# Two engines for one subtraction: every second half unit of split weights moves from VectorE to GpSimd in three stages of a two-model kernel

## The chip, the cores and the metric

The kernel is one program on one core of a Trainium2 chip. It is written in a tile language: the code names tiles and engines, and a scheduler then sets the order in which each engine gets its instructions. The metric is device time in microseconds for one execution, lower is better. Before the change the median of three runs is 2018.29 us (2015.76 to 2020.21).

In the text PE is TensorE (matrix multiplies), DVE is VectorE, ACT is ScalarE, POOL is GpSimd and SP is the engine that issues the DMAs. "L108" is line 108 of the kernel before.

## What is computed

Two small transformer networks run one behind the other, each with two layers, width 1024, 256 tokens, batch 1, all in float32. Only `x` of both is returned. Cut to its skeleton:

```
first block (x and a context ctx, modulated by c):
  layer 0: short convolution mixer on x and ctx, then SwiGLU FFN (hidden 2816) on x and ctx
  layer 1: neighbourhood attention of x (16 heads, bias, plus all of ctx), then SwiGLU FFN on x
second block (on the x above, with a memory of 256 rows):
  layer 0: FFN1 (x + 0.5 swiglu), mixer A (gated linear attention, 4 heads, plus 4 memory heads), FFN2
  layer 1: FFN1,                  mixer B (windowed attention, 16 heads, plus 4 memory heads), FFN2
```

Every one of these stages is a few products `activations @ weights`, and the weights are read from HBM as the stage needs them (345.68 MB are read in all).

## The kernel before

**Split products.** A float32 product is made of three fast passes. Every operand is split in two parts: `hi` is the value rounded to the fast format (`F32R`), `lo` is what is left. A product is then hi·hi + hi·lo + lo·hi. In the mixers and the attention `mm3` (L249, L250, L251) issues these three matmuls; in the FFNs `pair_unit` (L318, L320) does the same with wider tiles.

**The weight stream.** `WeightStream` brings the weights in units of 128 partitions x 1024 columns. `load` (L91) issues the DMA of a unit into one of five buffers `wraw`. `_split` makes the two parts: ACT copies `wraw` to `whi` (L107), and VectorE subtracts `whi` from `wraw` and writes `wlo` (L108). There are four buffers of each. `take` hands out a unit and first splits every unit up to two ahead of the one that is now used. The unit is cut into pieces of `self.width` columns; the FFN function `ffn_pairs` sets `width` to 1024 (one piece) and sets it back to 512 (two pieces, the two half units of the title) at its end. The stages with half units that matter here are the attention (`attention_block`), mixer A (`mixer_a`) and mixer B (`mixer_b`).

**What else VectorE does in these three stages.** It makes the `lo` part of every activation (`Net.split`, L264 and L267), normalises heads (`head_rstd` and `newton`: a reduction at L1022 and then a chain of a dozen instructions on 8 to 16 columns, L277 to L281; `head_scale`, L1042), finds the row maxima of the scores (L1150, L1826), scales the softmax rows (L1157, L1388, L1846) and adds the products to the residual `X` (L562, L1424, L1438). PE transposes what comes out of these (L1092 for queries, L1632 and L1853 for others), so PE waits for VectorE at those points.

**What sets the order.** In each of the three stages two generators are woven together by `weave`: one issues the projections (weights), the other the heads. From the program that comes out, the scheduler then makes one list per engine. Engines work their lists in order and wait for each other by semaphores. GpSimd has almost nothing in its list: it clears a few tiles (`memset`), among them at the start of mixers A and B (L1464 to L1471, L1707 to L1714).

Of the kernel before, what the change touches and what calls it, by code (L numbers as in the profile page):

```python
# [8 lines left out]
F32 = mybir.dt.float32  # L9
# [3 lines left out]
ALU = mybir.AluOpType  # L13
# [54 lines left out]
class WeightStream:  # L68
# [4 lines left out]
    def __init__(self, net, es, specs, raw_bufs, split_bufs, ahead):  # L73
# [10 lines left out]
        self.ready = []  # L84
        self.width = 512

    def load(self, upto):
        while self.loaded < min(upto, len(self.specs)):
            ap, nk, ncol, _ = self.specs[self.loaded]
            raw = self.raw_pool.tile([P, self.UNIT], F32, name="wraw", tag="raw")  # L90
            self.nc.sync.dma_start(raw[:, : nk * ncol].rearrange("p (k c) -> p k c", k=nk), ap)  # L91
            self.raw.append((raw, nk, ncol))
            self.loaded += 1

    def _split(self):
        self.load(self.split + self.raw_bufs)
        raw, nk, ncol = self.raw.pop(0)
        n = nk * ncol
        v = lambda t: t[:, :n].rearrange("p (k c) -> p k c", k=nk)
        if self.specs[self.split][3]:  # L100
            self.ready.append((v(raw), None, nk, ncol))
        else:
            hi = self.split_pool.tile([P, self.UNIT], F32R, name="whi", tag="hi")
            lo = self.split_pool.tile([P, self.UNIT], F32R, name="wlo", tag="lo")
            for c0 in range(0, n, self.width):
                cs = slice(c0, min(n, c0 + self.width))
                self.nc.scalar.copy(hi[:, cs], raw[:, cs])  # L107
                self.nc.vector.tensor_tensor(lo[:, cs], raw[:, cs], hi[:, cs].bitcast(F32), ALU.subtract)  # L108
            self.ready.append((v(hi), v(lo), nk, ncol))
        self.split += 1  # L110

# [51 lines left out]
class Net:  # L163
# [463 lines left out]
    def ffn_pairs(self, hp, x2, rows, evac, first):  # L627

        nc = self.nc
        s2 = hp.tile([P, HB, 2, T], F32R, name="s2")
        wide = lambda tag, bufs: hp.tile([P, 4, T], F32, name=tag, tag=tag, bufs=bufs)
        two = lambda t: t.rearrange("p (c t) -> p c t", c=2)
        self.half_banks(first)
        self.ws.width = WeightStream.UNIT
        env = {}

        def hidden(g, ps):

            low = wide("low", 1)
            nc.scalar.copy(low, ps[:, :, 1, :])
            h = wide("h", 2)
            nc.vector.tensor_tensor(h, ps[:, :, 0, :], low, ALU.add)
            if rows is not None:
                nc.vector.tensor_tensor(h, h, env["R"][:, None, :].to_broadcast([P, 4, T]), ALU.mult)
            yield
            sg = two(self.tmp())
            nc.scalar.activation(sg, h[:, 0:2, :], AF.Silu)
            s = two(self.tmp())  # L650
            nc.vector.tensor_tensor(s, h[:, 2:4, :], sg, ALU.mult)
            yield
            self.split(s2[:, 2 * g : 2 * g + 2, 0, :], s2[:, 2 * g : 2 * g + 2, 1, :], s)
            yield

        behind = iter(())
        ps = self.group_banks()
        for g in range(HB // 2):
            after = None
            for u in range(4):  # L660
                unit = self.ws.take()
                self.pair_unit(unit, [ps[:, u // 2 * 2 + c] for c in range(2)], x2, u % 2 * 4, KB)
                next(behind, None)
                if g == 0 and u == 1:
                    after = self.group_banks()
                    if rows is not None:
                        env["R"] = rows(after[:, 0].rearrange("p a t -> p (a t)"))
            behind = hidden(g, ps)
            next(behind)
            if g < HB // 2 - 1:  # L670
                ps = after if after is not None else self.group_banks()
        for j in range(4):
            if j % 2 == 0:
                i = self.turn
                self.turn = 1 - i
                self.open_half(i, "po")
            pss = [self.pg[i].tile([P, 2, T], F32, name="po", tag="po") for _ in range(2)]
            done = 0
            while done < HB:
                unit = self.ws.take()  # L680
                self.pair_unit(unit, pss, s2, done, HB)
                next(behind, None)
                done += unit[2]
            for c in range(2):
                evac(2 * j + c, pss[c])
        self.ws.width = 512
# [359 lines left out]
def attention_block(net):  # L1046

    nc, tc, a = net.nc, net.tc, net.a
    xh, xl = net.xa
    k8 = list(range(8))  # L1050
    net.ctx_pool.close()
    net.banks(3, 5)
    with ExitStack() as es:
        op = es.enter_context(tc.tile_pool(name="attn1", bufs=1))
        heads_pool = es.enter_context(ExitStack())
# [390 lines left out]
def mixer_a(net, x2, acc, gain):  # L1446
    nc, tc = net.nc, net.tc
    xh, xl = x2[:, :, 0, :], x2[:, :, 1, :]
    net.banks(4, 4)
    k8 = list(range(8))  # L1450
    with tc.tile_pool(name="mixa", bufs=1) as mp:
        yh = mp.tile([P, 12, T], F32R, name="yh")
# [236 lines left out]
def mixer_b(net, x2, acc, gain):  # L1689
    nc, tc = net.nc, net.tc  # L1690
    xh, xl = x2[:, :, 0, :], x2[:, :, 1, :]
    net.banks(4, 4)
    with tc.tile_pool(name="mixb", bufs=1) as mp:
        yh = mp.tile([P, 12, T], F32R, name="yh")
        yl = mp.tile([P, 12, T], F32R, name="yl")
# [191 lines left out]
def network(tc, a, out, es):  # L1887
# [27 lines left out]
    net.open_x = open_x  # L1915
    net.next_x = next_x
    x2, acc = attention_block(net)
    net.rope = net.cp.tile([P, 32], F32, name="rope")
    x2, acc = ffn2(net, x2, acc, net.p("mix_g0"), 1, rope=True)
    x2, acc = mixer_a(net, x2, acc, net.p("ffn2_g0"))  # L1920
    x2, acc = ffn2(net, x2, acc, net.p("ffn1_g1"), 0)
    x2, acc = ffn2(net, x2, acc, net.p("mix_g1"), 1)
    x2, acc = mixer_b(net, x2, acc, net.p("ffn2_g1"))
    ffn2(net, x2, acc, None, 0, last=True)

# [110 lines left out]
```

## Time and profile before

The times are those of the profiled execution. The span is what the profiler saw; the execution itself took 2018.19 us, 1.89 us more than its span.

| | value |
|---|---|
| median of three runs | 2018.29 us |
| profiled execution, its own time | 2018.19 us |
| its span | 2016.3 us |
| PE busy | 1992.2 us (99%) |
| DVE busy | 1497.7 us (74%) |
| ACT busy | 1025.2 us (51%) |
| POOL busy | 5.1 us (0%) |
| TensorE clock granted | 0.999 |
| moved from HBM | 345.68 MB at a mean of 172 GB/s |

The share of an engine over the whole span hides stages of different kind: the convolution block lies before 602 us, the attention at 602 to 834 us, mixer A at 1198 to 1342 us, mixer B at 1707 to 1835 us, and FFNs between them and after. In rows that tell who waited, "PE pa L1092 <- DVE t L1042: 2.4, 2, 1.2" reads: PE stood idle ahead of the instruction of line 1092 until the DVE instruction of line 1042 had ended; 2.4 us in total, 2 times, the longest 1.2 us.

### The profile page before, as it was taken

Reading aid. Unit: us, or ns where it says so; the run is one execution under the profiler, and the core shown is the slowest. Engines: PE = TensorE matmul, PEld = TensorE weight load, DVE = VectorE, ACT = ScalarE, POOL = GpSimd, SP = SyncE. Lnnn points to the kernel's source line nnn. Section 1 sums busy time; section 2 is a strip of 40 time slices with the busy share of each in tenths; the row PEclk is TensorE's granted clock in tenths of the full one; section 3 lists DMA queues with packets and bytes.
Section 4 is the critical chain, followed back from the end, with each engine's and each line's share of the span. In section 5 each row is a group of like instructions: output and inputs, shape, how many; then the busy total and the mean of one; then the engine's idle time right before and its main releaser. Section 6 shows DMA issues by size and latency. Waiting matters only on the chain. (4 is left out here: it accounts for less than half of the span.)

```text
span 2016.3 us, 32186 instructions
## 1 busy us (share of the span) xinstructions
PE 1992.2 (99%) x12454; PEld 1763.9 (87%) x12454; DVE 1497.7 (74%) x2626; ACT 1025.2 (51%) x1681; POOL 5.1 (0%) x26
## 2 busy tenths in 40 slices
PE   9999999999999999999999999999999999999999
PEld 6788988888899999888888899998888888988888
DVE  5898777767478779766687767787767776888774
ACT  4433532123355656655455547655555555675552
POOL 0000000000000000000000000000000000000000
PEclk9999999999999999999999999999999999999999
DMA  7665455667354334566666565556566656425654
GB/s 252 218 195 182 126 185 170 195 233 249 117 182 127 90 118 125 158 193 188 190 186 193 180 188 136 153 175 195 187 183 198 189 178 188 142 79 177 188 179 136
DMA packets 319273, 348.84 MB, mean 173 GB/s; under 512 B 12624, under 2 KB 307664, under 8 KB 319120
## 3 DMA queue, kind: packets, MB, share of 16 engines
q1 hardware_dynamic: 319120, 346.78, 55.8%
q8 instruction: 98, 1.61, 0.3%
q14 instruction: 55, 0.45, 0.1%
HBM read 345.68 MB, written 1.05 MB: 172 GB/s over the span
## 5 line engine op out<-in xcount | busy, mean ns | idle before, releaser
L108 DVE TENSOR_TENSOR wlo<-wraw,whi 128x512 fp32r<-128x512 f32 (+1 forms) x777 | 702.5, 918 | 341.3 <-ACT whi L107 336.3
L107 ACT CAST whi<-wraw 128x512 fp32r<-128x512 f32 (+1 forms) x777 | 608.9, 804 | 678.6 <-issue 182.9
L318 PE MATMUL pg<-x,whi 128*128 128x512 f32 x1408 | 383.7, 394 | 0.8 <-DVE x L267 0.8
L318 PEld LDWEIGHTS pg<-x,whi 128*128 128x128 f32 x1408 | 239.3, 188 | 33.3 <-DVE x L267 3.2
L318 PE MATMUL po<-s,whi 128*128 128x512 f32 x880 | 241.7, 393 | 0.0
L320 PEld LDWEIGHTS pg<-x,wlo 128*128 128x128 f32 x1408 | 213.5, 188 | 29.4
L320 PE MATMUL pg<-x,wlo 128*128 128x256 f32 x1408 | 219.7, 278 | 0.0
L249 PE MATMUL pm<-xh,whi 128*128 128x512 f32 (+1 forms) x576 | 217.8, 380 | 1.0 <-ACT xh L263 1.0
L250 PE MATMUL pm<-xl,whi 128*128 128x512 f32 (+1 forms) x576 | 217.6, 378 | 0.0
L251 PE MATMUL pm<-xh,wlo 128*128 128x512 f32 (+1 forms) x576 | 217.4, 378 | 0.0
L486 DVE SCALAR_TENSOR_TENSOR ada_acc<-wraw,sil,ada_acc 128x1024 f32<-128x1024 f32 x112 | 140.8, 1280 | 38.9 <-DMA wraw<-in_w_ada 38.3
L318 PEld LDWEIGHTS po<-s,whi 128*128 128x128 f32 x880 | 148.0, 188 | 17.2
L320 PEld LDWEIGHTS po<-s,wlo 128*128 128x128 f32 x880 | 136.4, 188 | 20.3
L320 PE MATMUL po<-s,wlo 128*128 128x256 f32 x880 | 140.9, 278 | 0.0
L249 PEld LDWEIGHTS pm<-xh,whi 128*128 128x128 f32 x576 | 108.1, 188 | 21.9 <-ACT xh L263 1.9
L250 PEld LDWEIGHTS pm<-xl,whi 128*128 128x128 f32 x576 | 108.4, 188 | 20.5 <-DVE xl L264 0.9
L251 PEld LDWEIGHTS pm<-xh,wlo 128*128 128x128 f32 x576 | 108.3, 188 | 19.9
L249 PE MATMUL pm<-sh,whi 128*128 128x256 f32 (+1 forms) x352 | 113.4, 322 | 0.0
L251 PE MATMUL pm<-sh,wlo 128*128 128x256 f32 (+1 forms) x352 | 113.2, 322 | 0.0
L250 PE MATMUL pm<-sl,whi 128*128 128x256 f32 (+1 forms) x352 | 112.7, 320 | 0.0
L251 PE MATMUL pm<-whi,xl 128*128 128x256 f32 x352 | 98.2, 279 | 0.0
L318 PE MATMUL pg<-xh,whi 128*128 128x512 f32 x352 | 96.0, 394 | 1.9 <-DVE xh L264 1.9
(442 smaller groups left out, 3391.1 us busy)
## 6 DMA issues: line engine op xcount, KB each, us to landing
wraw<-in_ffn_w_in SPq DMA_DIRECT2D x264, 512.0 KB, 3.7
wraw<-in_ffn_w_out SPq DMA_DIRECT2D x128, 512.0 KB, 3.5
wraw<-in_w_ada SPq DMA_DIRECT2D x96, 512.0 KB, 4.7
wraw<-in_a_w_in SPq DMA_DIRECT2D x28, 512.0 KB, 3.7
wraw<-in_attn_w_qkv SPq DMA_DIRECT2D x24, 512.0 KB, 4.1
wraw<-in_conv_w_in SPq DMA_DIRECT2D x18, 512.0 KB, 3.9
wraw<-in_ffn_w_out SPq DMA_DIRECT2D x28, 256.0 KB, 2.8
wraw<-in_b_w_in SPq DMA_DIRECT2D x14, 512.0 KB, 3.8
```

The source lines that it names most:

```text
L107: self.nc.scalar.copy(hi[:, cs], raw[:, cs])
L108: self.nc.vector.tensor_tensor(lo[:, cs], raw[:, cs], hi[:, cs].bitcast(F32), ALU.subtract)
L249: mm(ps, ah, bh, start=first, stop=False)
L250: mm(ps, ah, bl, start=False, stop=False)
L251: mm(ps, al, bh, start=False, stop=last)
L318: self.nc.tensor.matmul(pss[c], hi[:, kk, cs], x2[:, done + kk], start=done + kk == 0, stop=False)
L320: self.nc.tensor.matmul(pss[c][:, 0, :], lo[:, kk, cs], x2[:, done + kk, 0, :], start=False, stop=done + kk == nblocks - 1)
L486: nc.vector.scalar_tensor_tensor(accs[v], w, c, accs[v], ALU.mult, ALU.add)
```

## The change

`WeightStream` gets a list `engines`, at first only VectorE. In `_split` the i-th piece of a unit is subtracted by `engines[i % len(engines)]`. The attention and both mixers set the list to VectorE and GpSimd; `ffn_pairs` sets it back to VectorE alone. With pieces of 512 columns a unit has two, so the first half stays on VectorE and the second goes to GpSimd.

```diff
@@ WeightStream.__init__
         self.width = 512
+        self.engines = [net.nc.vector]
@@ WeightStream._split
-            for c0 in range(0, n, self.width):
+            for i, c0 in enumerate(range(0, n, self.width)):
                 cs = slice(c0, min(n, c0 + self.width))
                 self.nc.scalar.copy(hi[:, cs], raw[:, cs])
-                self.nc.vector.tensor_tensor(lo[:, cs], raw[:, cs], hi[:, cs].bitcast(F32), ALU.subtract)
+                self.engines[i % len(self.engines)].tensor_tensor(lo[:, cs], raw[:, cs], hi[:, cs].bitcast(F32), ALU.subtract)
@@ Net.ffn_pairs
         self.ws.width = WeightStream.UNIT
+        self.ws.engines = [nc.vector]
@@ attention_block
     net.banks(3, 5)
+    net.ws.engines = [nc.vector, nc.gpsimd]
@@ mixer_a and mixer_b
     net.banks(4, 4)
+    net.ws.engines = [nc.vector, nc.gpsimd]
```

The lines added shift the numbers: L108 is L110 in the changed kernel, L264 is L266, L277 to L281 are L279 to L283, L1022 is L1025, L1042 is L1045, L1846 is L1852.

What the scheduler makes of it: VectorE's list gets 106 instructions shorter, GpSimd's gets 106 subtractions. PE has the same 12314 rows of matmul in another order at some places of these three stages, ACT the same rows with some order changed, and SP three pairs of DMAs exchanged.

GpSimd's list from its first memset to the start of mixer A, in the changed kernel (`wlo`, `wraw`, `whi` are the lo part, the loaded weights and the hi part; `rb` is cleared in mixer A):

```order
L802 MEMSET z_118 128x516
L802 MEMSET z_119 128x516
L110 ISA
L110 TENSOR_TENSOR wlo<-wraw,whi 128x512 x2
L1065 MEMSET bias 128x256
L110 TENSOR_TENSOR wlo<-wraw,whi 128x512 x39
L1469 MEMSET rb 64x256
```

The 41 subtractions up to here are those of the attention and the first of mixer A; before the change only the memsets were in this list. The instruction `ISA` ahead of the first subtraction is new too. The list at mixer B, in the changed kernel:

```order
L110 TENSOR_TENSOR wlo<-wraw,whi 128x512 x40
L1713 MEMSET vh 128x1024
L1713 MEMSET vl 128x1024
L1720 MEMSET pth_17428 128x2x128
L1720 MEMSET ptl_17430 128x2x128
L1720 MEMSET pth_17429 128x2x128
L1720 MEMSET ptl_17431 128x2x128
L110 TENSOR_TENSOR wlo<-wraw,whi 128x512 x25
```

The 25 subtractions of mixer B stand behind the six memsets; all but one of the 40 ahead of them belong to mixer A.

VectorE's list in the attention, where the queries of one quarter of the heads are normalised (`qr_s`, `qr_g`, `qr_t`, `qr_r` are the statistics of the heads, `ptl` the lo part of the softmax rows of another quarter), before:

```order
L1022 TENSOR_REDUCE qr_s<-t 128x8
L108 TENSOR_TENSOR wlo<-wraw,whi 128x512
L1025 TENSOR_SCALAR qr_s<-qr_s 128x8
L108 TENSOR_TENSOR wlo<-wraw,whi 128x512
L277 TENSOR_SCALAR qr_g<-qr_s 128x8
L264 TENSOR_TENSOR ptl<-pa,pth 128x4x128
L279 SCALAR_TENSOR_TENSOR qr_t<-qr_g 128x8
L280 TENSOR_TENSOR qr_t<-qr_t,qr_s 128x8
L281 SCALAR_TENSOR_TENSOR qr_g<-qr_t,qr_g 128x8
```

and in the changed kernel:

```order
L1025 TENSOR_REDUCE qr_s<-t 128x8
L110 TENSOR_TENSOR wlo<-wraw,whi 128x512
L1028 TENSOR_SCALAR qr_s<-qr_s 128x8
L279 TENSOR_SCALAR qr_g<-qr_s 128x8
L281 SCALAR_TENSOR_TENSOR qr_t<-qr_g 128x8
L266 TENSOR_TENSOR ptl<-pa,pth 128x4x128
L282 TENSOR_TENSOR qr_t<-qr_t,qr_s 128x8
L283 SCALAR_TENSOR_TENSOR qr_g<-qr_t,qr_g 128x8
```

One of the two subtractions that stood inside the chain from L1022 to L281 is gone from VectorE's list, and the `ptl` split stands one step later.

VectorE's list in mixer B, at the first softmax rows (`bst` holds the row statistics, `t` the rows that PE transposes next), before:

```order
L108 TENSOR_TENSOR wlo<-wraw,whi 128x512
L1846 TENSOR_SCALAR t<-t,bst 128x128 x2
L108 TENSOR_TENSOR wlo<-wraw,whi 128x512
L1424 TENSOR_TENSOR X<-pm,X 128x512
L1838 TENSOR_TENSOR bst<-bst 128x4
L108 TENSOR_TENSOR wlo<-wraw,whi 128x512
L1839 RECIPROCAL bst<-bst 128x4
L264 TENSOR_TENSOR ptl_17430<-pa,pth_17428 128x384
L1846 TENSOR_SCALAR t<-t,bst 128x128 x2
```

and in the changed kernel:

```order
L1428 TENSOR_TENSOR X<-pm,X 128x512
L1852 TENSOR_SCALAR t<-t,bst 128x128 x2
L110 TENSOR_TENSOR wlo<-wraw,whi 128x512
L1844 TENSOR_TENSOR bst<-bst 128x4
L1845 RECIPROCAL bst<-bst 128x4
L1852 TENSOR_SCALAR t<-t,bst 128x128 x2
```

Between the first and the second pair of L1846 there stood two subtractions, one addition to `X` and one `ptl` split; now one subtraction stands there.

More of the change, by code (lines that the diff above doesn't have):

```diff
@@ L1692, in mixer_b @@
     net.banks(4, 4)
+    net.ws.engines = [nc.vector, nc.gpsimd]
     with tc.tile_pool(name="mixb", bufs=1) as mp:
```

## The prediction

> **What bounds the kernel now.** I read the page first, then the waits of PE by stage, then the windows of the three stages that the change touches.
>
> ```profile
> span 2016.3 us, 32186 instructions
> PE 1992.2 (99%) x12454; PEld 1763.9 (87%) x12454; DVE 1497.7 (74%) x2626; ACT 1025.2 (51%) x1681; POOL 5.1 (0%) x26
> ```
>
> PE works for 1992.2 of 2016.3 us, and the change takes no matmul away. So all that any change on VectorE can win is in the 24.1 us in which PE stands. How much of that lies in the three stages is told by the windows (columns: window, its length, then the busy time of PE, PEld, DVE, ACT and POOL with their instructions, the granted clock, the DMA share, GB/s), here the attention, mixer A and mixer B:
>
> ```profile
> 602.00:834.00 232.00, 224.57 (x1858) 213.17 (x1856) 188.01 (x508) 142.14 (x295) 0.31 (x1) 1.00 0.38 115
> 1198.00:1342.00 144.00, 141.82 (x1182) 137.93 (x1181) 115.72 (x322) 91.57 (x205) 0.71 (x13) 1.00 0.54 158
> 1707.00:1835.00 128.00, 122.82 (x1012) 115.92 (x1010) 110.73 (x375) 88.93 (x230) 2.85 (x6) 0.99 0.39 119
> ```
>
> PE stands 7.43, 2.18 and 5.18 us there, 14.8 us together: 0.73% of the span is the ceiling. VectorE is busy for 81, 80 and 87% of these stages. What PE waited for, in the same three windows and in the same order (line, then whose end released it: us in total, times, the longest):
>
> ```profile
> PE pa L1092 <- DVE t L1042: 2.4, 2, 1.2
> PE pg L318 <- DVE xh L264: 1.9, 2, 1.7
> PE pa L381 <- DVE acc L574: 0.8, 1, 0.8
> PE pa L1167 <- DVE rc_g L281: 0.6, 1, 0.6
> PE pm L250 <- DVE wlo L108: 0.5, 1, 0.5
> PE pa L1277 <- DVE t L1042: 0.3, 1, 0.3
> PE pa L1118 <- DVE t L1042: 0.2, 1, 0.2
> ...
> PE pa L1632 <- DVE t L1626: 1.8, 4, 0.8
> PE pa L1396 <- DVE t L1388: 0.2, 1, 0.2
> ...
> PE pm L249 <- ACT yh L263: 1.5, 3, 0.7
> PE pa L1853 <- DVE t L1846: 1.3, 1, 1.3
> PE pa L1853 <- ACT t L1844: 1.0, 2, 0.8
> PE pa L1785 <- DVE t L1742: 0.6, 1, 0.6
> PE pa L1396 <- DVE t L1388: 0.2, 1, 0.2
> PE pg L318 <- DVE x L267: 0.2, 1, 0.2
> ```
>
> VectorE is named for 6.7 + 2.0 + 2.3 = 11.0 us. The subtraction itself (`wlo`) is named once, for 0.5 us. The rest is other work of VectorE that came late, and the subtractions matter only because they stand in front of it.
>
> **What the change removes.** These are the subtractions of half units, on VectorE, in the three windows:
>
> ```profile
> L108 DVE TENSOR_TENSOR wlo<-wraw,whi 128x512 fp32r<-128x512 f32 x79 | 52.6, 685 | 7.1 <-ACT whi L107 6.8
> ...
> L108 DVE TENSOR_TENSOR wlo<-wraw,whi 128x512 fp32r<-128x512 f32 x79 | 52.9, 686 | 9.4 <-ACT whi L107 9.0
> ...
> L108 DVE TENSOR_TENSOR wlo<-wraw,whi 128x512 fp32r<-128x512 f32 x51 | 34.0, 685 | 1.4 <-ACT whi L107 1.2
> ```
>
> 106 of them leave VectorE's list, 0.686 us each: 72.7 us of VectorE's 414 us in these stages. How one of them lies on the path is seen at a stall of PE in the attention, first VectorE's own instructions in order of time (start, duration), then the PE row that ended the stall:
>
> ```profile
> 688.61 0.69 DVE L1022 TENSOR_REDUCE qr_s<-t 128x8 f32<-128x512 f32 x1 [0.41 <-ACT t L1021]
> 689.21 0.68 DVE L108 TENSOR_TENSOR wlo<-wraw,whi 128x512 fp32r<-128x512 f32 x1
> 689.81 0.17 DVE L1025 TENSOR_SCALAR qr_s<-qr_s 128x8 f32<-128x8 f32 x1
> 689.89 0.69 DVE L108 TENSOR_TENSOR wlo<-wraw,whi 128x512 fp32r<-128x512 f32 x1
> 690.49 0.17 DVE L277 TENSOR_SCALAR qr_g<-qr_s 128x8 int32<-128x8 int32 x1
> ...
> 693.79 0.63 PE L1092 MATMUL pa<-kc,t 128*128 128x128 f32 x4 [1.21 <-DVE t L1042]
> ```
>
> VectorE runs without a gap from 688.61 to the `t` that PE waits for. Two subtractions stand in it; the list of the changed kernel keeps one. So this stall would go from 1.21 to about 0.5 us if nothing else happened. I count the same for each stall that VectorE causes: 0.69 us, or the whole stall where it is shorter. Attention: 1.4 + 0.9 + 0.7 + 0.6 + 0.5 + 0.3 + 0.2 = 4.6. Mixer A: 1.7 + 0.2 = 1.9. Mixer B: 0.7 + 0.6 + 0.2 + 0.2 = 1.7. Together **8.2 us, the gain if GpSimd's work were free**. The 2.5 us for which PE waits for ACT in mixer B stay.
>
> **What the change adds.** 106 subtractions on GpSimd. The trace has no two-input instruction of GpSimd; its nearest row is a memset of the same size:
>
> ```profile
> L799 POOL MEMSET z<- 128x516 f32 x2 | 1.0, 528 | 0.3 <-POOLq L2032 0.3
> ```
>
> A memset passes the tile once, in 0.53 us. A subtraction passes it three times (two reads, one write). So 0.53 us is the lower bound and 3 x 0.53 = 1.58 us the upper; I take two passes, 1.06 us, between them and above VectorE's own 0.686, because reading and writing may overlap but two reads on one engine less so. 106 x 1.06 = 112 us on an engine that is otherwise idle (0.31, 0.71 and 2.85 us in the windows), so by itself this costs nothing. The Trainium skill, "GPSIMD Engine Reference", section 3.1, gives about 2.6 cycles per element at 1.2 GHz for a two-input operation; an estimate from that page is 512 x 2.6 / 1.2 GHz = 1.11 us, and the forecast below would move by 0.3 us.
>
> Is the second half of a unit late at PE? Units are split two ahead; 79 pieces, that is about 40 units, in 232 us make 5.9 us per unit, so a half unit has some 11 us until PE needs it, and in mixer B (51 pieces in 128 us) some 10 us. Against this stand 1.06 or 1.58 instead of 0.69 us: nothing. The one wait that the change puts in front of subtractions is at the head of mixer B, where 25 of them are queued behind six memsets that wait for the FFN's last matmul and take 2.85 us; that too is inside 10 us. A `wraw` buffer is free at most 0.9 us later for its next DMA on SP's queue; DMAs are busy for 38 to 54% there, and five buffers cover it. `ISA` and the first use of GpSimd come in the 600 us in which it idles. If such cover were gone, each late unit would cost PE its lateness, 0.4 to 0.9 us. The scheduler also puts some matmuls, DMAs and ACT copies in another order; the trace has no price for that, and I bound it by the longest stall, 1.7 us, on either side, and take 0.
>
> **The open cost: do the two engines hinder each other?** In the trace GpSimd never reads while VectorE works. Let f be the part of GpSimd's time for which VectorE stands still because of it; f is between 0 and 1. Then a moved subtraction gives VectorE 0.69 - f x 1.06 us. I take the middle, f = 0.5, since no row leans to either end: 0.16 us, 23% of full relief. The Trainium skill, "SBUF — State Buffer", section "Who interferes with whom", speaks against the change: a VectorE instruction with two SBUF inputs and a GpSimd instruction that reads SBUF exclude each other for the whole instruction. No row here shows that yet. Half-unit subtractions, `newton` steps and `acc` additions are of that kind, while the splits from PSUM banks (`pa`, `pm`) are not, so by that page f is well above 0 and below 1.
>
> Where f is large, the loss comes in the stretches in which VectorE has no room, or in which PE already stands (the windows as above, then for `wlo` alone: length, PE, PEld, DVE, clock, DMA share, GB/s):
>
> ```profile
> 770.00:810.00 40.00, 38.66 (x314) 35.78 (x314) 38.94 (x120) 25.98 (x55) 0.00 (x0) 1.00 0.44 135
> 1736.00:1768.00 32.00, 31.64 (x269) 30.71 (x268) 31.34 (x96) 21.67 (x50) 0.00 (x0) 1.00 0.44 134
> 1768.00:1800.00 32.00, 28.11 (x222) 24.05 (x221) 26.68 (x124) 25.53 (x86) 0.00 (x0) 0.95 0.21 66
> ...
> 770.00:810.00 40.00, 18.59 (x66) 12.39 (x66) 14.56 (x22) 1.00 0.44 135
> 1736.00:1768.00 32.00, 17.73 (x64) 11.95 (x64) 11.53 (x17) 1.00 0.44 134
> 1768.00:1800.00 32.00, 5.81 (x21) 3.76 (x20) 3.94 (x6) 0.95 0.21 66
> ```
>
> VectorE is busy 38.94 of 40 and 31.34 of 32 us in the first two, and 45 subtractions lie in the three; about 22 move.
>
> **The sum.** The profiled execution took 2018.19 us with a span of 2016.3; 1.89 us lie around the span and stay, and it stands 0.1 us below the median of the runs (2018.29), so I use it for both. 23% of 8.2 us is 1.9 us: 2018.2 - 1.9 = **2016.3 us**.
>
> **The rivals.** *Full relief* (f below 0.33): at f = 0 the whole 8.2 us come, 2010.0 us; at f = 0.33 half of it, 2014.2. For it speaks that no row quoted here shows one engine stretching another's instruction; against it that the moved half runs on GpSimd just when the `newton` steps behind the kept half run on VectorE. Its middle is 2012.
>
> *VectorE stands behind GpSimd* (slower): the break-even is f = 0.69/1.06 = 0.65. Above it each of the 22 moved subtractions in the full stretches lengthens VectorE, one for one on PE: at f = 1 by 0.37 us, 8.2 us in all, 2026.4 us; from f = 0.82 on it is 4 us. If a subtraction took 1.58 us as well, it would be 22 x 0.89 = 19.6 us, 2037.8. For it speaks that the two full stretches have no reserve; against it that a subtraction of GpSimd would have to stop VectorE for four fifths of its time. Its middle is 2024.5.
>
> *Late halves*: the second half of a unit reaches PE after PE needs it. At 0.37 us for each of 106, 39 us: 2057 us. The 10 us of lead speak against it.
>
> *The change does nothing*: the units could have been split whole, at width 1024. The lists show that 106 halves move, so this is left with next to nothing; 2018.2 us.
>
> **Chances.** Forecast (f from 0.33 to 0.82) 0.46, full relief 0.29, VectorE behind GpSimd 0.21, late halves 0.03, nothing done 0.01. What a measurement can tell from no change is 0.2%, 4.0 us: faster is below 2014.25, slower above 2022.3. So faster 0.29, same 0.47, slower 0.24. The likeliest case alone spans 2014.3 to 2022.3 us. The range that should hold the time 8 times in 10 reaches down to full relief and up past the middle of the slower rival: 2010 to 2025 us.
>
> **What would show it.** In the changed profile: 106 rows of L110 on POOL of about 1.06 us (0.53 to 1.58). L110 on DVE still 0.685 us on average if f is small; a longer mean of L110, of the small `newton` steps (0.17 us) and of L364 in these stages alone, or gaps ahead of them with no releaser, is f at work. PE's wait at L1092 near 0.5 us each is full relief; 1.2 or more is not. PE waiting at L250 for `wlo` on POOL would be late halves. DVE busy in the three windows falls from 414 us to about 342 if nothing is stretched. The forecast is wrong if PE's idle time in the three windows leaves the stretch of 11 to 19 us.

## The result and the profile after

The changed kernel takes 2064.48 us (2062.95 to 2068.61, five runs) against 2015.84 us for the kernel before, run beside it: a ratio of 1.0238 with a 95% interval of 1.0227 to 1.0248. It is 48.6 us slower. The prediction was 2016.3 us, with a range of 2010 to 2025. One of the four runs of mixer_a_alone, an experiment below, fell at a granted clock of 0.847 and took 2192.46 us; its time is left out there.

The page of the changed kernel first:

```profile
span 2065.3 us, 32437 instructions
PE 2010.8 (97%) x12454; PEld 1779.1 (86%) x12454; DVE 1497.1 (72%) x2520; ACT 1025.2 (50%) x1681; POOL 148.9 (7%) x132
```

VectorE has 106 instructions less and is as busy as before (1497.1 against 1497.7 us). PE has the same 12454 instructions and is busy for 18.6 us more. The stretches of the three stages, their ends placed where the same work stands (attention, mixer A, mixer B; columns as in the prediction), and the sum that the view gives below them:

```profile
602.00:850.15 248.15, 229.65 (x1866) 216.99 (x1864) 191.18 (x470) 142.92 (x296) 55.77 (x41) 0.98 0.36 109
1214.10:1381.61 167.51, 150.94 (x1184) 145.06 (x1182) 113.98 (x282) 91.83 (x205) 53.92 (x53) 0.94 0.46 136
1746.56:1884.01 137.45, 125.75 (x1011) 119.87 (x1010) 109.67 (x349) 88.97 (x230) 37.48 (x32) 0.95 0.36 111
sum 553.11, PE 506.34 PEld 481.92 DVE 414.83 ACT 323.71 POOL 147.17; mean PE 168.78 PEld 160.64 DVE 138.28 ACT 107.90 POOL 49.06
```

The three stages grew by 16.2, 23.5 and 9.5 us, 49.1 together: all of the loss, the largest part in mixer A, where VectorE had been the least full (80%). PE stands for 553.11 - 506.34 = 46.8 us there instead of 14.8 (32.0 more) and works for 506.34 instead of 489.21 us on the same matmuls, but for a handful at the edges (17.1 more), at a granted clock of 0.94 to 0.98 instead of 0.99 to 1.00. Both parts need an explanation.

What PE waits for in the whole of the changed kernel, the longest sums:

```profile
PE pa L1637 <- DVE t L1631: 12.1, 4, 3.9
PE pa L1096 <- DVE t L1045: 5.4, 4, 1.8
PE pa L1400 <- DVE t L1392: 3.9, 2, 3.2
...
PE pm L252 <- DVE wlo L110: 1.5, 2, 0.9
```

The tiles are named as before, and only the lines have moved. L1637 was L1632, with 1.8 us in four waits; L1096 was L1092, with 2.4 in two; L1400 was L1396, with 0.4. These are transposes of what VectorE makes at the end of a chain of small steps.

The subtractions, on GpSimd in the groups of the page, on VectorE in the stretch from 598 to 1890 us:

```profile
L110 POOL TENSOR_TENSOR wlo<-wraw,whi 128x512 fp32r<-128x512 f32 x106 | 144.0, 1360 | 1717.9 <-ACT whi L109 1162.2 <-PE po L322 371.9 <-PE pm L252 57.0
...
L110 DVE TENSOR_TENSOR wlo<-wraw,whi 128x512 fp32r<-128x512 f32 x124 | 90.2, 729 | 37.1 <-ACT whi L109 34.0 <-PE pm L251 2.1 <-issue 0.4
```

One takes 1.36 us on GpSimd. The kept ones went from 0.685 to 0.729 us, which alone would be little. What happened is seen in time order at the longest stall, in mixer A. These are rows of VectorE from the statistics of a head (`hst`) through the `newton` steps (`hn_`) to the rows `t` (start, duration), then the three GpSimd subtractions in the same time, then the PE row that waited:

```profile
1275.69 0.69 DVE L110 TENSOR_TENSOR wlo<-wraw,whi 128x512 fp32r<-128x512 f32 x1
1276.30 1.25 DVE L1623 TENSOR_TENSOR hst<-hst,qs 128x2 f32<-128x2 f32 x1
1277.59 0.16 DVE L1624 SCALAR_TENSOR_TENSOR hst<-hst 128x2 f32<-128x2 f32 x1
1277.79 1.26 DVE L1625 TENSOR_TENSOR hst<-hst 128x2 f32<-128x2 f32 x1
1279.09 0.17 DVE L1626 TENSOR_SCALAR hst<-hst 128x2 f32<-128x2 f32 x1
...
1281.46 0.16 DVE L283 SCALAR_TENSOR_TENSOR hn_g<-hn_t,hn_g 128x2 f32<-128x2 f32 x1
1281.66 1.12 DVE L281 SCALAR_TENSOR_TENSOR hn_t<-hn_g 128x2 f32<-128x2 f32 x1
...
1283.41 0.88 DVE L1631 SCALAR_TENSOR_TENSOR t<-pa,hst,og 128x256 f32<-128x256 f32 x2
...
1276.15 1.38 POOL L110 TENSOR_TENSOR wlo<-wraw,whi 128x512 fp32r<-128x512 f32 x1 [3.85 <-PE pm L253]
1277.75 1.29 POOL L110 TENSOR_TENSOR wlo<-wraw,whi 128x512 fp32r<-128x512 f32 x1 [0.21 <-DVE hst L1624]
1281.51 1.26 POOL L110 TENSOR_TENSOR wlo<-wraw,whi 128x512 fp32r<-128x512 f32 x1 [2.47 <-ACT whi L109]
...
1284.04 0.66 PE L1637 MATMUL pa<-kc,t 128*128 128x128 f32 x2 [3.88 <-DVE t L1631]
```

Steps on 128x2 elements that take 0.16 us take 1.25, 1.26 and 1.12 us, and each ends within 0.02 us of the end of a GpSimd subtraction (1277.53, 1279.04, 1282.77). VectorE shows as busy in that time, but it stands. I call this a hold. Three holds make this chain 3.1 us longer, and PE waits 3.88 us at its end. The Trainium skill, "SBUF — State Buffer", section "Who interferes with whom", describes it: an instruction of one engine fully blocks that of the other. This trace agrees.

That VectorE's busy time stayed the same because its steps became longer is also seen in the mean durations of its groups. Set beside the same groups of the kernel before, from 598 us to the end of mixer B, its steps are some 55 us longer in all: 20 us in TENSOR_TENSOR, 18 in SCALAR_TENSOR_TENSOR, 17 in TENSOR_SCALAR, and 0.1 us or less in reductions and reciprocals.

### The profile page after: what moved, and what is told of

Read it like the earlier page. It is cut to its first block, busy times and chain, and to the rows that moved or that the text cites. A ratio compares the mean times of both kernels' runs of the same rounds, so it can differ in the third digit from the quotient of the medians.

```text
span 2065.3 us, 32437 instructions
## 1 busy us (share of the span) xinstructions
PE 2010.8 (97%) x12454; PEld 1779.1 (86%) x12454; DVE 1497.1 (72%) x2520; ACT 1025.2 (50%) x1681; POOL 148.9 (7%) x132
## 4 chain that ended last, share of the span: by engine, by line
PE 52%; DVE 7%; ACT 2%; issue 1%; DMA 0%; POOL 0%; SPq 0%; ACTq 0%; DVEq 0%
PE pg L320 19%; PE po L320 10%; PE pg L322 10%; PE po L322 5%; PE pm L251 2%; PE pm L252 2%; PE pm L253 2%; DVE wlo L110 1%; PE pa L253 1%; PE pa L251 1%; PE pa L252 1%; ACT t L1842 1%; ACT whi L109 0%; DVE x L269 0%; DVE X L564 0%
## 5 line engine op out<-in xcount | busy, mean ns | idle before, releaser
L110 DVE TENSOR_TENSOR wlo<-wraw,whi 128x1024 fp32r<-128x1024 f32 (+1 forms) x671 | 638.7, 963 | 349.4 <-ACT whi L109 342.6
L110 POOL TENSOR_TENSOR wlo<-wraw,whi 128x512 fp32r<-128x512 f32 x106 | 144.0, 1360 | 1717.9 <-ACT whi L109 1162.2
```

Of the source, the lines that this page charges most:

```text
L110: self.engines[i % len(self.engines)].tensor_tensor(lo[:, cs], raw[:, cs], hi[:, cs].bitcast(F32), ALU.subtract)
```

## The experiments

In all of them but one, a table fixes the order of every engine's instructions, so that PE, ACT and SP work through the list of before or of the changed kernel exactly; mixer_a_alone has the scheduler's own order. All differences below are to the median of the kernel before that ran beside them (2016.4 to 2018.1 us). "Busy" is VectorE's busy time from the page.

| run | what it does | us | difference | ratio, 95% interval | VectorE busy |
|---|---|---|---|---|---|
| order_before | the change, in the order of before | 2048.78 | +30.7 | 1.0151 [1.0132, 1.0169] | 1497.8 |
| order_after | VectorE does all, in the order of the change | 2033.33 | +15.3 | 1.0083 [1.0066, 1.0100] | 1501.2 |
| memset_second_half | GpSimd only writes zeros, order of before | 2011.72 | -6.4 | 0.9969 [0.9959, 0.9980] | 1444.9 |
| mixer_a_alone | the change in mixer A alone | 2039.65 | +21.6 | 1.0110 [1.0093, 1.0126] | not read |
| memset_order_after | zeros, order of the change | 2014.32 | -3.1 | 0.9985 [0.9975, 0.9994] | 1447.0 |
| copy_order_before | GpSimd copies once | 2013.09 | -4.3 | 0.9983 [0.9974, 0.9993] | 1452.6 |
| short_subtract | GpSimd subtracts half the columns | 2019.95 | +3.6 | 1.0018 [1.0009, 1.0027] | 1465.3 |
| two_copies | GpSimd copies twice | 2022.41 | +6.0 | 1.0033 [1.0019, 1.0048] | 1469.8 |
| two_pieces | GpSimd subtracts in two pieces | 2037.41 | +21.0 | 1.0105 [1.0087, 1.0123] | 1487.3 |
| selective | GpSimd subtracts 60 of the 106 | 2028.03 | +11.7 | 1.0060 [1.0045, 1.0075] | 1491.4 |
| copy_extra | VectorE does all, GpSimd copies too | 2025.66 | +8.3 | 1.0048 [1.0035, 1.0062] | 1511.7 |
| late_subtractions | VectorE does all, behind chains | 2053.19 | +35.8 | 1.0178 [1.0163, 1.0193] | 1501.5 |
| gpsimd_behind_chains | GpSimd does 106, behind chains | 2072.45 | +55.1 | 1.0278 [1.0262, 1.0294] | 1500.2 |
| subtractions_out_of_chains | VectorE does all, 46 out of chains | 2022.60 | +5.2 | 1.0026 [1.0015, 1.0037] | 1498.9 |

### The engine or the order

The scheduler made a new order when the subtractions moved. Four runs take the two apart, and one looks at one stage. The edit that fixes the order is one call; `pinned` (not shown) reads the table and ties each instruction to the one that stands ahead of it on its engine:

```diff
         network(tc, a, out, es)
+        pinned(tc)
```

The text set off below each name is what was expected of that run before it ran. `order_before`:

> The changed kernel with the instruction order of the kernel before: PE, ACT and SP work the very same lists as before, VectorE works its list of before without the 106 second halves, GpSimd has these 106 in its list. So the hardware side of the change is there and the scheduler's new order is not. Theory H (GpSimd's subtractions hold up VectorE's small two-input instructions, which stand on the chains that PE waits for): close to the changed kernel, 2050 to 2065 us, VectorE's busy time about 1497 us as there. Theory O (the new order alone costs: transposes stand earlier in PE's list and less other work covers the wait): back near the kernel before, 2010 to 2022 us.

`order_after`:

> The kernel before (VectorE does all subtractions) with the order of the changed kernel on PE, ACT and SP, and the same order of everything on VectorE except the 106 second halves, which the scheduler fits in. So the new order is there and GpSimd does nothing. Theory H: near the kernel before, 2014 to 2026 us. Theory O: the loss is here, 2045 us or more.

`memset_second_half` is order_before with another instruction on GpSimd; `memset_order_after` is the same in the order of the changed kernel:

```diff
-                self.engines[i % len(self.engines)].tensor_tensor(lo[:, cs], raw[:, cs], hi[:, cs].bitcast(F32), ALU.subtract)
+                if i % len(self.engines):
+                    self.nc.gpsimd.memset(lo[:, cs].bitcast(F32), 0.0)
+                else:
+                    self.nc.vector.tensor_tensor(lo[:, cs], raw[:, cs], hi[:, cs].bitcast(F32), ALU.subtract)
```

`memset_second_half`:

> As the kernel with the order of before and GpSimd in it, but GpSimd clears the second half of each lo part instead of subtracting: it writes and reads nothing. Left out is the lo part of these half units. Theory H: without GpSimd's reads VectorE is not held up, its busy time falls by 73 us to about 1425 us, and PE's stalls that VectorE causes shrink by the 8 us of my sum: 2008 to 2014 us. Theory O: the same as the kernel with the order of before, whatever that is. If writing alone holds VectorE up, it stays near the changed kernel.

`memset_order_after`:

> All engines work in the order of the changed kernel, pinned, but GpSimd writes zeros into the second half of lo instead of subtracting (leaves out the true lo of these 106 half units). A memset reads nothing. In the order of before this gave 2011.7 us. Theory A, the order of the changed kernel costs some 15 us by itself, whatever GpSimd does: 2011.7 + 15 = 2027 us (2022 to 2031). Theory B, that order is bad only where VectorE or the memory ports are loaded by the subtractions, and free without them: 2012 to 2016 us.

Neither part explains the loss alone: order_before (2048.8) came out just below the 2050 to 2065 us of theory H, order_after (2033.3) above its 2026 and below the 2045 of theory O. GpSimd's subtractions cost 30.7 us in the order of before, the new order costs 15.3 us with VectorE doing all; 46.0 together, against 48.6 measured. The order is not bad in itself: beside memsets it costs about 3 us (2014.32 against 2011.72, with intervals that touch). It costs 15 us wherever VectorE is not truly relieved, with all subtractions back on VectorE (15.3) or with GpSimd's holds (2064.5 - 2048.8 = 15.7; 48.6 - 30.7 = 17.9 by the differences to the kernels before that ran beside each). In order_after the 106 subtractions went where the scheduler fitted them in, so that part is in its 15 us too. Its longest waits are those of the changed kernel:

```profile
PE pa L1632 <- DVE t L1626: 5.9, 4, 1.7
PE pa L1092 <- DVE t L1042: 3.6, 3, 1.2
PE pa L1396 <- DVE t L1388: 3.5, 3, 2.5
```

The two parts also differ in kind: on their pages PE is busy for 2002.0 us in order_before, 9.8 more than before, and for 1992.2 us in order_after, as before. So the loss of the order alone is standing, while the holds also make PE's work longer (the last section shows how).

The memset run shows full relief. VectorE's busy time in the three stretches, in the sum row of the same view (602.00 to 830.08, 1195.60 to 1336.90, 1701.91 to 1828.51 us):

```profile
sum 495.98, PE 485.37 PEld 464.57 DVE 360.22 ACT 320.99 POOL 57.44; mean PE 161.79 PEld 154.86 DVE 120.07 ACT 107.00 POOL 19.15
```

It falls from 414.46 to 360.22 us, by 0.51 us for each moved subtraction, less than its duration of 0.69 us, because neighbours overlap: in the rows of the prediction a subtraction of 0.68 us at 689.21 is followed by the next step at 689.81. (On the pages, where no end of a stretch matters, it is 52.8 us, 0.50 for each.) The memset run came out where theory H had it in time, 2011.7 us, but not in busy time, 1444.9 us against some 1425. These 54 us off VectorE are worth 6.4 us of time. In the changed kernel VectorE is at 414.83 again: 54.6 us of holds, 38% of GpSimd's 144.0 us (by the pages 52.2 us, 36%).

`mixer_a_alone`:

> The change in mixer A alone, VectorE alone in attention and mixer B, with the scheduler's own order. In the changed kernel mixer A lasts 164.7 us from its first matmul to the first of the FFN behind it, 141.2 before: 23.5 us of the 49 us. If the stages add up, 2016 + 23.5 = 2039.5 us, 2036 to 2043. If the three stages' losses hang together (clock, order), it differs from that by more than 5 us.

+21.6 us in mixer A alone, within the expected 2036 to 2043 us: its share in the full change (23.5 us between the stretches) stands without the other stages.

### Kind of instruction or time of holding

Two inputs, or simply the time? GpSimd is given other work on the same half units, in the order of before. Each fence shows what stands in place of the `memset` line of the edit above. `copy_order_before`:

```diff
+                    self.nc.gpsimd.tensor_copy(lo[:, cs], raw[:, cs])
```

> Order of before, pinned; GpSimd copies the loaded half unit into lo (one input read, one write) instead of subtracting (leaves out the true lo of these 106 half units). Theory A, any GpSimd instruction that reads holds VectorE for its length: the subtraction cost 37 us more than the memset (2048.8 against 2011.7) for 145.7 us of GpSimd's time, 0.25 us for each; a copy lies between the memset's 0.53 and the subtraction's 1.37 us, about 0.75, so 80 us x 0.25 = 20 us: 2032 us (2024 to 2042), and VectorE's steps of 0.16 us are stretched to the copy's length at most. Theory B, only an instruction with two inputs hinders: 2011 to 2014 us, no step stretched.

`short_subtract`:

```diff
+                    h = slice(cs.start, cs.start + 256)
+                    self.nc.gpsimd.tensor_tensor(lo[:, h], raw[:, h], hi[:, h].bitcast(F32), ALU.subtract)
+                    self.nc.gpsimd.memset(lo[:, h.stop : cs.stop].bitcast(F32), 0.0)
```

> Order of before, pinned. GpSimd subtracts only the first 256 of the 512 columns of a second half unit and writes zeros into the others (leaves out the true lo of these 256 columns). So it reads two inputs as in the change, but for about half the time, some 0.7 us, as long as the copy of copy_order_before (0.64 us, 2013.1 us). Theory A, the time for which GpSimd holds VectorE decides, whatever it does: 2011 to 2019 us. Theory B, two inputs hinder and one does not: about half of the 37 us of the whole subtraction, 2024 to 2034 us.

`two_copies`:

```diff
+                    self.nc.gpsimd.tensor_copy(lo[:, cs], raw[:, cs])
+                    self.nc.gpsimd.tensor_copy(lo[:, cs], raw[:, cs])
```

> Order of before, pinned. GpSimd copies the loaded half unit into lo twice, one copy behind the other (leaves out the true lo of these 106 half units): one input per instruction, 2 x 0.64 = 1.29 us per half unit, nearly the 1.37 us of the subtraction. Theory A, the time for which GpSimd holds VectorE decides: 2035 to 2050 us, and VectorE is busy for some 1490 us again. Theory B, one input hinders little: 2012 to 2019 us.

`two_pieces`:

```diff
+                    for h in (slice(cs.start, cs.start + 256), slice(cs.start + 256, cs.stop)):
+                        self.nc.gpsimd.tensor_tensor(lo[:, h], raw[:, h], hi[:, h].bitcast(F32), ALU.subtract)
```

> Order of before, pinned. GpSimd subtracts the whole second half unit, as in the change, but in two instructions of 256 columns, about 0.7 us each. Theory A, the sum of the holding time decides: 2043 to 2058 us, as in order_before (2048.8). Theory B, the length of one hold decides, since a step of VectorE can go between the two pieces: 2015 to 2032 us.

The single copy hit theory B in time (2013.1), but its steps show theory A at work: some of 0.16 us take up to 0.58 us, nearly the copy's own 0.64. Steps of the same chain, two in the copy run and then the first of them beside the memsets, where it is not stretched (nanoseconds: shortest, median, longest):

```profile
L1626 DVE TENSOR_TENSOR hst<-hst,qs x4: 161/256/566, 1251.7 to 1305.3; 128x2 f32<-128x2 f32 x4
L282 DVE TENSOR_SCALAR hn_g<-hst x4: 164/170/581, 1253.7 to 1306.1; 128x2 int32<-128x2 int32 x4
```

```profile
L1626 DVE TENSOR_TENSOR hst<-hst,qs x4: 151/160/161, 1252.4 to 1304.4; 128x2 f32<-128x2 f32 x4
```

So an instruction with one input can hold too. The cost rises with the sum of the holds, which is VectorE's busy time above the 1444.9 us of the memset run:

| GpSimd's work | holds, us | cost beside the memsets, us | cost per us of hold |
|---|---|---|---|
| one copy | 7.7 | 2.1 | 0.27 |
| subtraction of half the columns | 20.4 | 10.0 | 0.49 |
| two copies | 24.9 | 12.4 | 0.50 |
| subtraction in two pieces | 42.4 | 27.4 | 0.65 |
| whole subtraction | 52.9 | 37.1 | 0.70 |

How much of GpSimd's time becomes a hold differs by the work: 11% of the 68 us of the single copies, 16% of the 157 us of two copies, 24 and 25% for the pieces of 256 columns (86 and 171 us), 36% of the 146 us of the whole subtraction. Why is not shown: the runs differ in inputs and length, and a copy also starts at another time, since it does not wait for the `whi` that ACT makes, as the subtraction mostly does.

The holds are the page's busy time less 1444.9, the costs the differences of the large table plus 6.4. The cost of one copy is a difference of two small ones, with some 3 us of uncertainty on its 2.1 us by their intervals; the costs from 10 us on are clear of that. short_subtract (2019.95) came out 1 us above theory A's range and 4 below theory B's. Two copies lie beside the subtraction of half the columns, with nearly the same holds and the same price, although one reads one input and the other two. Neither theory's number for two_copies (2035 to 2050, 2012 to 2019) held: I had counted GpSimd's time, and the copies took 157 us of it; what they held is half of what the subtractions held in 146 us. Two pieces hold less than one (42.4 against 52.9 us) and cost 9.7 us less, between the two theories: length matters somewhat, but a step that slips in between does not save the chain.

### Room or place

The price rises with the amount, from 0.27 to 0.70 us of time per us of hold, while a us of relief gave 0.12. Is that because VectorE runs out of room, or because of where the holds fall? `copy_extra`:

```diff
-                self.engines[i % len(self.engines)].tensor_tensor(lo[:, cs], raw[:, cs], hi[:, cs].bitcast(F32), ALU.subtract)
+                if i % len(self.engines):
+                    self.nc.gpsimd.tensor_copy(lo[:, cs], raw[:, cs])
+                self.nc.vector.tensor_tensor(lo[:, cs], raw[:, cs], hi[:, cs].bitcast(F32), ALU.subtract)
```

> Order of before, pinned, and VectorE subtracts all half units as before the change. In addition GpSimd copies the loaded half unit into lo ahead of VectorE's subtraction, which overwrites it: 106 copies of 0.64 us that hold VectorE without relieving it of anything. In copy_order_before the same copies held VectorE by some 8 us and cost 1.4 us beside the memsets, while VectorE was relieved of 53 us. Theory A, a hold costs little as long as VectorE has room and much where it has none: VectorE has no room here, so 8 us of holds cost 0.6 to 0.7 us each, 4 to 8 us: 2021 to 2027 us. Theory B, short holds are harmless in themselves: 2016 to 2019 us.

2025.66 us: the number of theory A, and theory B is out. Without relief the copies add 14.0 us to VectorE's busy time (1511.7 against 1497.7) and 8.3 us to the time, 0.59 us per us, where with relief they cost 0.27. VectorE's subtraction now also has to wait for the copy into the same tile, but in the trace it does so once, for 0.4 us. This fits that room decides how much of a hold reaches PE; with the uncertainty of the 0.27 it is not proof.

`selective` (shortened; `FREE` is the list of the 60):

```diff
+                eng = self.engines[i % len(self.engines)]
+                if i % len(self.engines):
+                    self.seconds += 1
+                    eng = eng if self.seconds - 1 in FREE else self.engines[0]
+                eng.tensor_tensor(lo[:, cs], raw[:, cs], hi[:, cs].bitcast(F32), ALU.subtract)
```

> Order of before, pinned; of the 106 second halves GpSimd subtracts 60, those beside which the trace of copy_order_before shows within 1.35 us from their start no step of VectorE that two inputs or a scaling from SBUF make holdable, other than a kept subtraction. The other 46 stay on VectorE. Theory A, the place decides (steps of chains that PE waits for): relief of 60/106 of the 6.5 us of memset_second_half and little hindrance, 2011 to 2020 us. Theory B, GpSimd's total time decides: 60/106 of the 31 us of order_before, 2031 to 2040 us.

2028.0 us, between the theories and nearer B. With 60 moved, relief is 60/106 of 52.8 us, and 1497.7 - 29.9 = 1467.8 us would be left without holds; 1491.4 were measured, 23.6 us of holds for 60 subtractions, 0.39 us each against 0.50 in order_before. Choosing them by the trace of another run avoided a fifth of the holds, not most. Probably the run's own times shift, and a subtraction that misses one step meets the next; this was not followed step by step.

`late_subtractions`:

> VectorE subtracts everything, as before the change, and PE, ACT and SP keep the order of before. Only VectorE's order is new: 124 of the 212 half-unit subtractions of the three stages, which stood ahead of or inside a chain of small steps that PE waits for (statistics of heads, softmax row scales), stand behind that chain, at most about 4 us later. Theory A, the stalls come from the place of the subtractions and the halves have some 10 us of lead: most of the 8.2 us of full relief come without a second engine, 2010 to 2014 us. Theory B, VectorE's sum of work sets the stalls: 2016 to 2020 us. Theory C, the halves come late at PE: above 2022 us, with PE waiting for wlo.

`gpsimd_behind_chains`:

> GpSimd does the 106 subtractions, with PE, ACT and SP in the order of before; VectorE's order is that of late_subtractions without the 106, and each GpSimd subtraction waits for the VectorE instruction that stands ahead of its place in that order. So GpSimd does the same work, but does not start inside a chain. In the order of before with GpSimd free to start at any time it was 2048.8 us. Theory A, the loss comes from chains of small steps that a subtraction of GpSimd holds up while PE waits for them: two thirds or more of the 31 us go, 2012 to 2028 us. Theory B, the loss goes by GpSimd's total time, wherever it lies: 2042 to 2052 us.

late_subtractions went as theory C had it, far above 2022 us; gpsimd_behind_chains met neither theory. What PE waits for, first in late_subtractions, then in gpsimd_behind_chains:

```profile
PE pm L250 <- DVE wlo L108: 7.7, 8, 3.2
...
PE pa L250 <- DVE wlo L108: 2.5, 1, 2.5
```

```profile
PE pm L252 <- POOL wlo L110: 12.2, 9, 4.3
...
PE pa L252 <- POOL wlo L110: 5.0, 1, 5.0
...
PE pa L1096 <- DVE t L1045: 1.6, 2, 0.8
...
PE pa L1637 <- DVE t L1631: 1.1, 2, 0.7
```

Behind the chains, the waits at the ends of two kinds of chain are small (1.6 and 1.1 us; 4.6 and 8.1 in order_before), as theory A says; a third, at L1400, is not (5.1 us; 4.1 in order_before), VectorE is as busy as there (1500.2 us), and the halves now reach PE late, by up to 5 us. These two runs therefore don't settle the price of a place: they trade one wait for another. They do show that the halves have far less reserve than I had worked out.

`subtractions_out_of_chains`:

> VectorE subtracts everything, and PE, ACT and SP keep the order of before. Of VectorE's list only this is new: 46 half-unit subtractions that stood inside a chain of small dependent steps (statistics of heads, row scales) stand behind the chain's last step, with no other work crossed, so 1 to 3 us later. Theory A, what stands inside these chains is what PE waits for: PE's waits at L1092 (2.4 us) and L1632 (1.8 us) shrink, 2012 to 2016 us. Theory B, the subtractions fill the time in which one small step waits for the one before it (a subtraction starts 0.08 us behind a small step, the next small step 0.20 us), so that VectorE has less room without them: 2017 to 2026 us.

2022.6 us, the number of theory B: even 46 subtractions, moved 1 to 3 us within VectorE's own list, make it 5 us slower. PE's waits did not shrink (L1092 from 2.4 to 3.1, L1632 from 1.8 to 3.0 us). That the overlap which B names is the reason is only argued: VectorE's busy time rose by just 1.2 us. So the runs fit that the room of VectorE matters; that a hold in a chain costs more than one elsewhere is seen at single stalls, and no run here separates it from the amount. No run here computed everything and was faster than before, and the memset run, which leaves work out, puts what this relief can bring, in the order of before, at 0.3%.

## Why the prediction was wrong

- **What bounds the kernel** was right: PE, with 14.8 us of standing in the three stages, and VectorE named for most of it. So was the size of **full relief**: 8.2 us worked out, 6.4 us measured with memsets (which hold a little themselves), 2010 against 2011.7. Per subtraction VectorE gained 0.51 us of busy time instead of the 0.686 that I took.
- **GpSimd's duration**: 1.36 us, within the bounds of 0.53 to 1.58, above the 1.06 that I took.
- **f** was taken as 0.5 for want of a row; it is 0.38, inside the forecast's own 0.33 to 0.82. Put into my own formula, the measured sizes give 0.51 - 0.38 x 1.36 = 0.0 us of relief per subtraction, 2018.2 us: still "no change". VectorE's busy time in the stages, 414.46 and 414.83 us, agrees with that to the microsecond. So it was not the size of these terms that failed.
- **The step that failed** is "a moved subtraction gives VectorE 0.69 - f x 1.06 us", used on PE's stalls as if relief and holds had one price. A us of relief is worth 0.12 us of time (6.4 of 54 us), probably because the list of before puts the subtractions where they cost PE little, and the sum is capped by the 14.8 us. A us of hold costs up to 0.70 us and has no such cap, since it comes when GpSimd happens to start, often on a step of 0.16 us in a chain that PE waits for. Equal amounts of both gave 37.1 - 6.4 = 30.7 us in order_before.
- **VectorE stands behind GpSimd** was the rival with the right sign, and a wrong condition and price: it was to come from f = 0.82 on, in 22 pieces of the full stretches, for 4 to 20 us. It came at f = 0.38, in all three stages, and cost most in mixer A, which was not among those stretches.
- **The order**, bounded by 1.7 us and taken as 0, was worth 15 to 18 us in the changed kernel. The bound, the longest stall of before, was no bound: an order made for a relieved VectorE makes its own stalls when the relief does not come.
- **The clock** was not in the sum. PE's longer work, 17.1 of the 49.1 us in the stages, is a cost that I had no term for (see the last section).
- **Late halves** hardly happened (one wait of 0.2 us for a `wlo` of GpSimd, two of 1.5 us together for one of VectorE), but their cover was over-rated: "10 us of lead" was an average over units, and 4 us of delay in late_subtractions already made PE wait 10 us for `wlo`.
- Of what was to show it, the idle time of PE in the three windows (46.8 us against "11 to 19") was the clear sign; VectorE's busy time, which was to fall to about 342 us if nothing is stretched, showed the holds (414.83).

## What to carry to other kernels

Before work moves from VectorE to GpSimd, ask whether the two read tiles in SBUF at the same time: busy time that stays the same although instructions left is a sign of holds, and short steps that end together with a GpSimd instruction show it. Don't net relief against hindrance: relief is worth only what waits in front of PE today, a hold lands on whatever chain runs just then. And price the new order that a scheduler makes as a change of its own, by running (as order_before and order_after do) the new engine in the old order and the old engine in the new one.

## What the hardware showed that I had not expected

**Which steps are held.** In order_before, VectorE's list is that of before without the 106. Five kinds of its steps there (nanoseconds: shortest, median, longest):

```profile
L279 DVE TENSOR_SCALAR kr_g<-kr_s x5: 176/1252/1257, 630.2 to 1754.6; 128x16 int32<-128x16 int32 x4, 128x4 int32<-128x4 int32 x1
...
L1161 DVE TENSOR_SCALAR t<-t,at_s x16: 476/480/1517, 640.0 to 787.3; 128x512 f32<-128x512 f32 x16
...
L1025 DVE TENSOR_REDUCE kr_s<-t x9: 420/678/686, 619.6 to 1752.5; 128x8 f32<-128x512 f32 x8, 128x4 f32<-128x256 f32 x1
...
L1157 DVE RECIPROCAL at_s<-at_s x32: 150/161/166, 639.8 to 792.9; 128x1 f32<-128x1 f32 x32
...
L1428 DVE TENSOR_TENSOR X<-pm,X x16: 678/689/694, 1327.1 to 1846.6; 128x512 f32<-128x512 f32 x16
```

Scalings of a tile from SBUF (TENSOR_SCALAR) are held up to 1.26 and 1.52 us although they read one tile; reductions, reciprocals and an addition with one input from a PSUM bank are not, in any of these rows. Beside the memsets scalings are still held, as this row of memset_second_half shows (L1164 is the same line), while steps with two inputs are not, as the row of L1626 above showed:

```profile
L1164 DVE TENSOR_SCALAR t<-t,at_s x16: 476/480/803, 637.6 to 780.9; 128x512 f32<-128x512 f32 x16
```

The Trainium skill's "SBUF — State Buffer", section "Who interferes with whom", covers these cases; the traces agree with each.

**A short stall slows PE afterwards.** The view by windows around the stall of 3.88 us in the changed kernel, in pieces of 3.41 us (the columns as before; the clock is the number ahead of the DMA share):

```profile
1275.93:1279.35 3.42, 3.42 (x33) 3.42 (x32) 3.32 (x6) 1.60 (x4) 2.67 (x2) 1.00 0.17 16
1279.35:1282.76 3.41, 0.81 (x8) 0.61 (x6) 3.24 (x11) 1.61 (x3) 1.25 (x1) 1.00 0.70 209
1282.76:1286.18 3.42, 2.14 (x10) 2.17 (x11) 2.07 (x8) 0.47 (x1) 0.01 (x1) 0.50 0.33 92
1286.18:1289.59 3.41, 3.41 (x16) 2.96 (x15) 1.69 (x5) 1.87 (x6) 0.00 (x0) 0.50 0.48 147
1289.59:1293.00 3.41, 3.41 (x18) 3.41 (x18) 2.44 (x5) 1.72 (x5) 1.28 (x1) 0.50 0.00 0
1293.00:1296.41 3.41, 3.41 (x31) 3.41 (x31) 1.25 (x4) 1.88 (x6) 1.07 (x1) 1.00 0.55 154
```

In a piece of 3.41 us PE stood for 2.6 us; in the next three pieces the granted clock is 0.50, and PE begins 16 and 18 matmuls in a piece instead of 31 to 33. The stall of 3.88 us thus costs several us more behind it. From the mean clocks of the three stages, 0.98, 0.94 and 0.95, (0.02 x 248.15 + 0.06 x 167.51 + 0.05 x 137.45) / 0.5 makes some 44 us at 0.50 there; by the 0.99 of mixer B before it was 0.01 x 128 / 0.5, some 3 us. The Trainium skill, "TensorE: Matmul & The Clock Gate", section "HAM oscillation — how this bites in real kernels", puts the limit at gaps of more than about 3.4 us. This stall of 3.88 us fits that, but shorter ones were enough too: the prediction's row 1768.00:1800.00 of the kernel before has a clock of 0.95, by which some 3 us ran at 0.50, and no wait of PE in its three windows is longer than 1.7 us. So here the measurement decides. Where exactly the limit lies was not measured.
